# Order of wide and narrow matrix products in the chunks of a projection

## The chip, the cores and the metric

The kernel runs on one core of a Trainium2 chip. The metric is the device time of one execution in microseconds. The kernel before takes 881.99 us, the median of three runs (881.4 to 882.06). All engines start together, each works through its own queue in order, and they wait for each other by semaphores: TensorE (PE; its loading of weights is shown as PEld), VectorE (DVE), ScalarE (ACT), GpSimd (POOL) and SyncE (SP), which issues the transfers.

## The reference

The reference is an encoder of two layers on 256 tokens of width 1024, in float32. Each layer has a token mixer and a gated MLP:

```
def _token_mixer(xn, ...):
    u, q, k, v, g_pool, g_attn = jnp.split(xn @ w_in, SPLITS, axis=-1)
    ...
    pool_out = jnp.einsum('bsgc,gcd->bsgd', pooled, w_pool).reshape(B, S, POOL_WIDTH) * pool_scale
    ...
    merged = jax.nn.sigmoid(g_pool) * (pool_out @ w_a) + jax.nn.sigmoid(g_attn) * (attn_out @ w_b)
    return merged @ w_o

def _conv_ffn(xn, w_up, conv_w, conv_b, w_down):
    a, gval = jnp.split(xn @ w_up, 2, axis=-1)
    ...
    return (jax.nn.gelu(a) * gval) @ w_down

for layer in range(DEPTH):
    h = h + _token_mixer(_rmsnorm(h, norm1[layer]), ...)
    h = h + _conv_ffn(_rmsnorm(h, norm2[layer]), ...)
return _rmsnorm(h, norm_f)
```

Nearly all the work is the products of the 256 tokens with the weights.

## The kernel before

Float32 products are made of reduced-precision ones. Every operand is split into a high part, rounded to the format that TensorE multiplies (`fp32r`), and a low part, what the rounding left. A product is then three: high weight by high operand, high weight by low operand, low weight by high operand.

**Weights.** The class `Weights` loads them from HBM in 1 MB tiles (`raw`, three buffers, SP's queue), and cuts each tile into two pieces. `open_next` splits a piece: ACT casts the raw piece to `wh` (L177), DVE subtracts to get `wl` (L178), each 128x1024. `wh` and `wl` have five buffers each, and a piece is split when the piece three before it is taken (`LOOK = 3`, in `get`). A buffer of `wh` is free again when the last product that reads it is done, one of `wl` likewise.

**Projections.** `proj` (L479) takes one piece, 128 output channels by 1024 inputs, and one PSUM buffer of four (`mm`). Its operand `x2` holds for each of eight groups of 128 input channels the high part of the 256 tokens and the low part next to each other, so one product of 512 columns makes the high and the low one at once. `two_sums` (L471) does the whole chunk: eight wide products, 128x512, with the high weights (L475), into both halves of the PSUM buffer, and then eight narrow ones, 128x256, with the low weights and the high part of the operand (L477), added to the second half:

```
for k in range(nk):
    nc.tensor.matmul(ps, wh(k), x2[:, k], start=(k == 0), stop=False)
for k in range(nk):
    nc.tensor.matmul(ps[:, 1], wl(k), x2[:, k, 0], start=False, stop=(k == nk - 1))
```

The first product of a sum writes the buffer (`start`), all others add. The two halves are added together when the sum is read: `add_up` (L497 on ACT, L498 on DVE), or the lines of the queries and keys (L957 to L969).

`two_sums` is called 224 times in all, 112 per layer: 96 times by `proj` with `nk = 8`, for the pooling input, queries and keys, the projection `w_a` (operand `po2`), the gates, and the two halves of the MLP's input; 8 times in `pool_out` with `nk = 2` (`pool_ps`); 8 times for `w_b` with `nk = 4` (`b_ps`).

**Other work on TensorE.** The values (`v_sum`) and the output projections (`residual_mm`, `res_ps`, L502 to L504) have the roles turned round: weights stream as 512 columns, and all their products are wide. The attention has small products: scores (`s_ps`, 256 and 128 columns), transposes of the softmax rows (`pt_ps`, L901, 128 columns) and the weighted values (`o_ps`). They are put between the chunks of the last queries and keys and of `w_a`.

**What sets the order.** The text of the kernel is the program order. A scheduler puts the instructions of each engine into that engine's queue, by its own estimate of when each could run, and adds the semaphores. So an edit on TensorE can also change the order in which casts, subtractions and evictions stand on ACT and DVE. Each queue is then worked off strictly in order.

Of the kernel before, what the change touches and what calls it, by code (L numbers as in the profile page):

```python
# [204 lines left out]
def encoder(ctx, tc, x, w_in, w_pool, pool_scale, w_a, w_b, w_o, norm1, norm2, w_up, conv_w,  # L205
            conv_b, w_down, rel_bias, norm_f, onehot, edges, out):
    nc = tc.nc
# [255 lines left out]
    def store(t, r, xn):  # L463
# [4 lines left out]
        nc.sync.dma_start(out=ov[:, t, 512:], in_=xn[:, 512:])  # L468
        yield

    def two_sums(ps, wh, wl, x2, nk):  # L471


        for k in range(nk):
            nc.tensor.matmul(ps, wh(k), x2[:, k], start=(k == 0), stop=False)  # L475
        for k in range(nk):
            nc.tensor.matmul(ps[:, 1], wl(k), x2[:, k, 0], start=False, stop=(k == nk - 1))  # L477

    def proj(x2):  # L479

        i, (wh, wl) = W.get()
        ps = mmp.tile([P, 2, S], F32, tag="mm", name="proj_ps")
        two_sums(ps, lambda k: wh[:, k, :], lambda k: wl[:, k, :], x2, KD)
        W.free(i)
        return ps[:, 0], ps[:, 1]

    def halves(a):

        return a.rearrange("p (t m) -> p t m", t=2)
# [74 lines left out]
    def v_tile():  # L564
        return acc.tile([P, 512], F32, tag="acc", name="v_ps")
# [11 lines left out]
    def two_parts(tag, name):  # L577


        return big.tile([P, KD, 2, 2, P], F32R, tag=tag, name=name)  # L580
# [123 lines left out]
    def first_values(rs, raw_x, fs, done, pe, keep_values):  # L704

        xuh, xul = raw_x
        x2 = two_parts("x", "x2")

        rows = mmp.tile([P, 2, P], F32, tag="mm", name="r_ps")
        with tc.issue_after(pe.ins):  # L710
            for t in range(2):
                nc.tensor.transpose(rows[:, t, :], rs[t][:, 0:1].to_broadcast([P, P]), ident)
        for k in range(0, KD, 2):
            f = fs[k // 4][:, k % 4 : k % 4 + 2]
            for j in range(2):
                nc.vector.scalar_tensor_tensor(
                    out=f[:, j], in0=f[:, j], scalar=gcol[:, k + j : k + j + 1], in1=rows,
                    op0=ALU.mult, op1=ALU.mult,
                )
            oh, ol = (x2[:, k : k + 2, part] for part in (0, 1))  # L720
            nc.scalar.copy(out=oh, in_=f)
            nc.vector.tensor_sub(out=ol, in0=f, in1=oh.bitcast(F32))
        ps = done
        for g in range(NG):
            held = [W.get() for _ in range(4)] if g + 1 < NG else []
            for t in range(2):
                keep_values(t, g, ps[t], rs)
            ps = [v_tile() for _ in range(2)]
            for t in range(2):
                for n, (_, (wh, wl)) in enumerate(held):  # L730
                    for j in range(2):
                        k = 2 * n + j
                        for m, (a, w) in enumerate(((xuh, wh), (xuh, wl), (xul, wh))):
                            nc.tensor.matmul(  # L734
                                ps[t], a[:, k, t, :], w[:, j, :], start=(k + m == 0),
                                stop=(k == KD - 1 and m == 2),
                            )
            for i, _ in held:
                W.free(i)
        return x2  # L740

    for l in range(DEPTH):
# [21 lines left out]
        if l == 0:  # L764
            with tc.manual_schedule():
                begun = begin_values_of_x()
            x2 = first_values(*begun, keep_values)
        else:
            for g in range(NG):
                held = begun[0] if g == 0 else [W.get() for _ in range(4)]  # L770
                for t in range(2):
                    if g + t == 0:
                        ps = begun[1]
                    else:
                        ps = v_tile()
# [17 lines left out]
        for gi in range(3, -1, -1):  # L793
            w = WINDOWS[gi]
# [7 lines left out]
            cur, n = u, S + 2 * PAD  # L802
            sh = 1
            while sh < w:
# [3 lines left out]
                    out=nxt[:, :, 0:n], in0=cur[:, :, 0:n], in1=cur[:, :, sh : sh + n]  # L808
# [7 lines left out]
            if hw > 1:  # L816
# [5 lines left out]
                out=pd, in0=cur[:, :, o : o + S], scalar=1.0 / w, in1=u[:, :, PAD : PAD + S],  # L822
# [8 lines left out]
        def pool_out(po2):  # L831
            for j in range(2):
                i, (wh, wl) = W.get()
                for gg in range(2):
                    for oc in range(2):
                        ps = mmp.tile([P, 2, S], F32, tag="mm", name="pool_ps")
                        cc = slice(oc * P, (oc + 1) * P)
                        two_sums(
                            ps, lambda k: wh[:, 2 * gg + k, cc], lambda k: wl[:, 2 * gg + k, cc],
                            pooled[2 * j + gg], 2,  # L840
                        )
                        c = 4 * j + 2 * gg + oc
                        sc = hps[:, l, c : c + 1]
                        po = sm.tile([P, 2, P], F32, tag="u", name="po")
                        nc.scalar.mul(out=po, in_=halves(ps[:, 1]), mul=sc)
                        nc.vector.scalar_tensor_tensor(
                            out=po, in0=halves(ps[:, 0]), scalar=sc, in1=po, op0=ALU.mult, op1=ALU.add
                        )
                        nc.scalar.copy(out=po2[:, c, 0], in_=po)
                        nc.vector.tensor_sub(out=po2[:, c, 1], in0=po, in1=po2[:, c, 0].bitcast(F32))  # L850
                    if gg:
                        W.free(i)
                    yield
# [76 lines left out]
        steps = []  # L930
# [10 lines left out]
        for m, c in enumerate(PAIRS):  # L941
# [7 lines left out]
            for n in range(4):  # L949
                if m == 1:  # L950
                    next(pool_parts)
                src, rest = (halves(a) for a in proj(x2))
                hd = 2 * c + n % 2
                scale = HD**-0.5 if n < 2 else 1.0
                if hd < HPG:
# [3 lines left out]
                        out=lo[:, hd], in0=src, scalar=scale, in1=hi[:, hd].bitcast(F32),  # L959
# [3 lines left out]
                        out=lo[:, hd], in0=rest, scalar=scale, in1=lo[:, hd].bitcast(F32),  # L963
                        op0=ALU.mult, op1=ALU.add,
                    )
                else:
# [3 lines left out]
                        out=o, in0=src, scalar=scale, in1=o, op0=ALU.mult, op1=ALU.add  # L970
# [20 lines left out]
        for c in range(KD):  # L991
            th = gate(c)
            nc.vector.scalar_tensor_tensor(
                out=pa[:, c, :], in0=th, scalar=1.0, in1=pa[:, c, :], op0=ALU.add, op1=ALU.mult
# [3 lines left out]
        for c4 in range(2):  # L998
            ths = [gate(4 * c4 + j) for j in range(4)]
            for j2 in range(2):  # L1000
                i, (wh, wl) = W.get()
                for j in range(2):
                    c = 4 * c4 + 2 * j2 + j
                    ps = mmp.tile([P, 2, S], F32, tag="mm", name="b_ps")
                    cc = slice(j * P, (j + 1) * P)
                    two_sums(ps, lambda k: wh[:, k, cc], lambda k: wl[:, k, cc], at2, 4)
                    m = sm.tile([P, S], F32, tag="u", name="m")
                    add_up(m, (ps[:, 0], ps[:, 1]))
                    nc.vector.scalar_tensor_tensor(
                        out=m, in0=ths[2 * j2 + j], scalar=1.0, in1=m, op0=ALU.add, op1=ALU.mult  # L1010
                    )
                    nc.vector.tensor_add(out=m, in0=m, in1=pa[:, c, :])
                    m = halves(m)
                    nc.scalar.copy(out=mh[:, c], in_=m)
                    nc.vector.tensor_sub(out=ml[:, c], in0=m, in1=mh[:, c].bitcast(F32))
                W.free(i)

        x2 = two_parts("x", "x2")
# [41 lines left out]
        held, ps = entry  # L1060
        first = keep_entry(ps)
        ps = v_tile()
# [70 lines left out]
        if l + 1 < DEPTH:  # L1133
            x2 = two_parts("x", "x2")
# [34 lines left out]
```

## Time and profile before

| | |
|---|---|
| time, median of three runs | 881.99 us |
| time of the profiled execution | 882.08 us |
| span in its profile | 880.3 us |
| TensorE busy | 872.4 us, 99% |
| weight loads busy | 757.5 us, 86% |
| DVE busy | 682.5 us, 78% |
| ACT busy | 525.6 us, 60% |
| GpSimd busy | 14.0 us, 2% |
| mean share of the transfer engines (q1) | 56.0% |
| granted TensorE clock | 0.999 |

A line of a group reads: line of the kernel, engine, operation, what is written and read with shapes, count; then busy time in us and the mean ns of one; then the idle time of the engine just before them and what ended most of it. A line of the timeline reads: start in us from the span's start, length in us, engine, line, operation, tiles, count; neighbouring instructions of the same line are merged to one. Products on TensorE overlap, so the length of one is more than the distance from its start to the start of the next.

### The profile page before, as it was taken

How to read it: one execution, taken by the hardware profiler on the slowest of the kernel's cores; microseconds unless marked ns; L12 is line 12 of the kernel's file. 1: busy time of each engine (PE TensorE's matmuls, PEld its weight loads, DVE VectorE, ACT ScalarE, POOL GpSimd, SP SyncE). 2: the span in 40 equal slices, each digit the busy share in tenths (PEclk: the TensorE clock that was granted, in tenths of full speed). 3: DMA queues.
4: the chain of work that ended last, by engine and by line, in shares of the span. 5: the costliest groups of instructions: out<-in, count | busy, mean ns of one | idle time of the engine just before them, and what ended most of it. 6: DMA issues, size and time to landing. Idle time of an engine off the chain costs nothing.

```text
span 880.3 us, 12800 instructions
## 1 busy us (share of the span) xinstructions
PE 872.4 (99%) x4817; PEld 757.5 (86%) x4817; DVE 682.5 (78%) x1167; ACT 525.6 (60%) x929; POOL 14.0 (2%) x40
## 2 busy tenths in 40 slices
PE   9999999999999999999999999999999999999996
PEld 7888889988888888888888888999888888888885
DVE  6988886767869987787755987776678698878774
ACT  6746654556648766666545574554566486666652
POOL 2000000000000000000000000000000000000000
PEclk9999999999999999999999999999999999999999
DMA  9669744455554665465636465443556447566541
GB/s 327 233 204 313 240 144 147 141 181 176 175 207 147 205 225 193 155 221 198 239 120 220 163 199 185 148 163 124 191 189 205 159 146 257 167 197 205 172 144 50
DMA packets 125791, 164.48 MB, mean 187 GB/s; under 512 B 2995, under 2 KB 106107, under 8 KB 125600
## 3 DMA queue, kind: packets, MB, share of 16 engines
q1 hardware_dynamic: 125712, 163.65, 56.0%
q8 instruction: 38, 0.62, 0.3%
q14 instruction: 25, 0.20, 0.1%
q10 hardware_dynamic: 16, 0.00, 0.0%
HBM read 162.57 MB, written 3.69 MB: 189 GB/s over the span
## 4 chain that ended last, share of the span: by engine, by line
PE 99%; ACT 0%; POOL 0%; DVE 0%; issue 0%; POOLq 0%; ACTq 0%
PE proj_ps L475 40%; PE proj_ps L477 21%; PE res_ps L502 6%; PE v_ps L572 6%; PE res_ps L503 6%; PE res_ps L504 6%; PE v_ps L734 2%; PE b_ps L475 2%; PE v_ps L647 1%; PE b_ps L477 1%; PE pool_ps L475 1%; PE o_ps L922 1%; PE s_ps L872 1%; PE pt_ps L901 1%; PE s_ps L867 1%; PE o_ps L918 1%
## 5 line engine op out<-in xcount | busy, mean ns | idle before, releaser
L178 DVE TENSOR_TENSOR wl<-raw,wh 128x1024 fp32r<-128x1024 f32 x274 | 334.2, 1223 | 132.8 <-ACT wh L177 128.2
L177 ACT CAST wh<-raw 128x1024 fp32r<-128x1024 f32 x274 | 286.0, 1049 | 189.4 <-PE proj_ps L475 128.4
L475 PE MATMUL proj_ps<-x,wh 128*128 128x512 f32 x1408 | 354.1, 393 | 0.0
L475 PEld LDWEIGHTS proj_ps<-x,wh 128*128 128x128 f32 x1408 | 254.1, 189 | 47.3 <-issue 0.5
L477 PEld LDWEIGHTS proj_ps<-x,wl 128*128 128x128 f32 x1408 | 192.0, 190 | 13.8
L477 PE MATMUL proj_ps<-x,wl 128*128 128x256 f32 x1408 | 196.3, 282 | 0.0
L502 PE MATMUL res_ps<-wh,actq 128*128 128x512 f32 (+1 forms) x184 | 70.2, 381 | 0.0
L503 PE MATMUL res_ps<-wl,actq 128*128 128x512 f32 (+1 forms) x184 | 70.1, 381 | 0.0
L504 PE MATMUL res_ps<-wh,actk 128*128 128x512 f32 (+1 forms) x184 | 69.9, 380 | 0.0
L504 PEld LDWEIGHTS res_ps<-wh,actk 128*128 128x128 f32 x184 | 34.6, 188 | 6.7
L502 PEld LDWEIGHTS res_ps<-wh,actq 128*128 128x128 f32 x184 | 34.7, 188 | 6.2
L503 PEld LDWEIGHTS res_ps<-wl,actq 128*128 128x128 f32 x184 | 34.7, 188 | 6.0
L475 PE MATMUL proj_ps<-po,wh 128*128 128x512 f32 x128 | 33.1, 400 | 0.0
L1099 ACT ACTIVATE y<-y 128x256 f32<-128x256 f32 x44 | 18.3, 416 | 24.7 <-DVE y L1096 24.5
L1082 ACT ACTIVATE y<-a,prm 128x256 f32<-128x256 f32 x36 | 21.6, 600 | 15.9 <-DVE a L498 15.9
L416 ACT ACTIVATE junk<-h 128x512 f32<-128x512 f32 (+1 forms) x20 | 10.9, 546 | 27.0 <-DVE h L414 27.0
L502 PE MATMUL res_ps<-wh,m 128*128 128x512 f32 (+1 forms) x72 | 26.5, 368 | 0.0
L475 PEld LDWEIGHTS proj_ps<-po,wh 128*128 128x128 f32 x128 | 22.9, 189 | 4.1
L503 PE MATMUL res_ps<-wl,m 128*128 128x512 f32 (+1 forms) x72 | 26.3, 366 | 0.0
L504 PE MATMUL res_ps<-wh,m 128*128 128x512 f32 (+1 forms) x72 | 26.3, 365 | 0.0
L572 PE MATMUL v_ps<-wh,x 128*128 128x512 f32 x80 | 25.7, 392 | 0.0
L1083 DVE SCALAR_TENSOR_TENSOR y<-a,prm,y 128x255 f32<-128x255 f32 x36 | 17.3, 480 | 8.1 <-ACT y L1082 8.1
(208 smaller groups left out, 1101.6 us busy)
## 6 DMA issues: line engine op xcount, KB each, us to landing
raw<-in_w_in_dram SPq DMA_DIRECT2D x58, 1024.0 KB, 5.7
raw<-in_w_up_dram SPq DMA_DIRECT2D x44, 1024.0 KB, 4.9
raw<-in_w_down_dram SPq DMA_DIRECT2D x22, 1024.0 KB, 4.7
raw<-in_w_a_dram SPq DMA_DIRECT2D x8, 1024.0 KB, 5.3
raw<-in_w_o_dram SPq DMA_DIRECT2D x8, 1024.0 KB, 4.9
raw<-in_w_b_dram SPq DMA_DIRECT2D x4, 1024.0 KB
sk<-fd SPq DMA_DIRECT2D x1, 2560.0 KB
raw<-in_w_pool_dram SPq DMA_DIRECT2D x2, 1024.0 KB
```

What stands on the lines that cost most here:

```text
L177: lambda: nc.scalar.copy(out=h, in_=src),
L178: lambda: nc.vector.tensor_sub(out=l, in0=src, in1=h.bitcast(F32)),
L475: nc.tensor.matmul(ps, wh(k), x2[:, k], start=(k == 0), stop=False)
L477: nc.tensor.matmul(ps[:, 1], wl(k), x2[:, k, 0], start=False, stop=(k == nk - 1))
L502: nc.tensor.matmul(ps, ah, wh, start=first, stop=False)
L503: nc.tensor.matmul(ps, ah, wl, start=False, stop=False)
L504: nc.tensor.matmul(ps, al, wh, start=False, stop=last)
L572: nc.tensor.matmul(ps, x2[:, 2 * n + j, part, t, :], w[:, j, :], start=(n + m == 0), stop=(n == 3 and m == 5),)
L734: nc.tensor.matmul(ps[t], a[:, k, t, :], w[:, j, :], start=(k + m == 0), stop=(k == KD - 1 and m == 2),)
L1082: nc.scalar.activation(y, a, AF.Identity, bias=b, scale=w1)
L1083: nc.vector.scalar_tensor_tensor(out=y[:, 1:], in0=a[:, : S - 1], scalar=w0, in1=y[:, 1:], op0=ALU.mult, op1=ALU.add)
L1099: nc.scalar.activation(y2, y2, AF.Tanh, scale=c)
```

## The change

Only `two_sums` is changed. A flag that lives outside it turns over with every call. In the first, third, fifth call the order is as before. In every second call the order is: the first wide product, which opens the sum, then all narrow ones, then the remaining wide ones. The products, their operands and the buffers are the same; the last product of the sum, which ends it, is a wide one in these calls. All products of both kinds now stand on one line, L484, and the lines below move by seven.

```diff
+    turns = {"rest": False}
+
     def two_sums(ps, wh, wl, x2, nk):
...
-        for k in range(nk):
-            nc.tensor.matmul(ps, wh(k), x2[:, k], start=(k == 0), stop=False)
-        for k in range(nk):
-            nc.tensor.matmul(ps[:, 1], wl(k), x2[:, k, 0], start=False, stop=(k == nk - 1))
+        steps = [(k, True) for k in range(nk)]
+        rests = [(k, False) for k in range(nk)]
+        steps = steps[:1] + rests + steps[1:] if turns["rest"] else steps + rests
+        turns["rest"] = not turns["rest"]
+        for n, (k, wide) in enumerate(steps):
+            out, w, x = (ps, wh, x2[:, k]) if wide else (ps[:, 1], wl, x2[:, k, 0])
+            nc.tensor.matmul(out, w(k), x, start=(n == 0), stop=(n == 2 * nk - 1))
```

## The prediction

> **What bounds the kernel now.** I read the page first: busy times, the chain that ended last, the costliest groups.
>
> ```profile
> PE 872.4 (99%) x4817; PEld 757.5 (86%) x4817; DVE 682.5 (78%) x1167; ACT 525.6 (60%) x929; POOL 14.0 (2%) x40
> ...
> PE 99%; ACT 0%; POOL 0%; DVE 0%; issue 0%; POOLq 0%; ACTq 0%
> ...
> L178 DVE TENSOR_TENSOR wl<-raw,wh 128x1024 fp32r<-128x1024 f32 x274 | 334.2, 1223 | 132.8 <-ACT wh L177 128.2
> L177 ACT CAST wh<-raw 128x1024 fp32r<-128x1024 f32 x274 | 286.0, 1049 | 189.4 <-PE proj_ps L475 128.4
> L475 PE MATMUL proj_ps<-x,wh 128*128 128x512 f32 x1408 | 354.1, 393 | 0.0
> ```
>
> The chain is TensorE from end to end, and the products sit behind no idle time: the last column of the L475 group is 0.0. So the end is the sum of the distances from one product's start to the next one's. The 393 ns is the length of one, not its distance: products overlap. Distances have to be read from starts, in the timeline of TensorE. This is the MLP stage, where a chunk is eight wide products (L475) and eight narrow ones (L477):
>
> ```profile
> 325.88 1.98 PE L475 MATMUL proj_ps<-x,wh 128*128 128x512 f32 x8
> 327.69 1.12 PE L477 MATMUL proj_ps<-x,wl 128*128 128x256 f32 x8
> 328.64 2.00 PE L475 MATMUL proj_ps<-x,wh 128*128 128x512 f32 x8
> 330.48 1.11 PE L477 MATMUL proj_ps<-x,wl 128*128 128x256 f32 x8
> ...
> 337.02 0.40 PE L502 MATMUL res_ps<-wh,actq 128*128 128x512 f32 x1
> ...
> 338.18 0.39 PE L504 MATMUL res_ps<-wh,actk 128*128 128x512 f32 x1
> ...
> 342.26 0.39 PE L504 MATMUL res_ps<-wh,actk 128*128 128x512 f32 x1
> ```
>
> The eight wide ones at 325.88 follow another wide one and take 327.69 - 325.88 = 1.81 us, 226.7 ns each in the unrounded starts. The next eight follow narrow ones and take 330.48 - 328.64 = 1.84. So a wide stretch costs 27 ns more behind narrow products. The residual rows show where: behind narrow ones the first five steps (337.02 to 338.18) take 1.16 us, 1.133 at the steady pace; the next 18 (to 342.26) take 4.08, which is 226.7 each. Unrounded, the surpluses of the first five are 6.5, 9, 1.5, 5.5 and 4.5 ns. A narrow stretch is the reverse: its first product is 113 ns from the second, the second 119, the rest 120; eight take 0.95 us.
>
> What happens behind few products of a kind, in the stage of the pooled projection and in that of the bias table:
>
> ```profile
> 79.26 0.62 PE L475 MATMUL pool_ps<-pl,wh 128*128 128x512 f32 x2
> 79.72 0.40 PE L477 MATMUL pool_ps<-pl,wl 128*128 128x256 f32 x2
> 79.96 2.00 PE L475 MATMUL proj_ps<-x,wh 128*128 128x512 f32 x8
> 81.80 1.12 PE L477 MATMUL proj_ps<-x,wl 128*128 128x256 f32 x8
> ```
>
> ```profile
> 44.80 1.11 PE L477 MATMUL proj_ps<-x,wl 128*128 128x256 f32 x8
> 45.84 0.28 PE L374 MATMUL f_ps<-onehot_r,rh 33*4 33x256 f32 x1
> ...
> 48.11 1.11 PE L477 MATMUL proj_ps<-x,wl 128*128 128x256 f32 x8
> 49.15 0.28 PE L374 MATMUL f_ps<-onehot_r,rh 33*4 33x256 f32 x1
> ```
>
> Two narrow products are enough for the full surplus: the wide eight at 79.96 take 1.84 again. Two wide ones behind narrow ones take 79.72 - 79.26 = 0.46, 0.453 at the steady pace: a short stretch pays only its own first positions. And eight narrow ones take 1.04 us to the next group whether one wide product stands before them (44.80) or eight (48.11).
>
> **The change part by part.** In every second sum the wide stretch of eight becomes one wide product, eight narrow, seven wide. Products, operands and bytes stay the same in number.
>
> *The pace of TensorE.* Two chunks in a row go from 8 wide, 8 narrow, 8 wide, 8 narrow to 8 wide, 8 narrow, 1 wide, 8 narrow, 7 wide, and the 7 run on into the next chunk's 8. The number of meetings of sizes is the same, but of two full wide stretches behind narrow ones (2 x 27.4 ns) one shrinks to a single product (6.5 ns): 21 ns less per pair. I counted the stretches in the two kernels' instruction lists, over proj_ps, pool_ps and b_ps. Wide stretches behind narrow, before: 166 of five or more (27.4 ns), 16 of four (22.3, the b_ps rows), 16 of two (12.6, mean of the pool_ps rows), 1 of one: 4.55 + 0.36 + 0.20 + 0.01 = 5.11 us. After: 110 of five or more, 4 of three (17), 105 of one (6.5): 3.01 + 0.07 + 0.68 = 3.76. That is -1.35 us. Stretches behind the 128-wide products of the attention (36 ns net for eight, 6 for one, 10 for two): eight full ones become single and two more of two appear, -8 x 36 + 8 x 6 + 2 x 10 = -0.22 us. Narrow stretches behind a wide product go from 229 to 243, each with 8 ns of quick start: -0.11. Eight more groups of 128-wide products stand behind a wide one, which costs about 12 ns in the starts: +0.10. Sum: **-1.6 us**.
>
> Unknown is the lone wide product between two narrow stretches; no 8-8-1-8 order is in the trace. Bound below: it runs at the steady pace, 105 x 6.5 = 0.7 us more gain, -2.3. Bound above: the narrow eight behind it lose their quick start, 112 x 8 = +0.9, so -0.7. I take the middle value, since the nearest rows (0.46 for two wide ones; 1.04 behind one wide or eight) show neither deviation.
>
> The Trainium skill, "TensorE: Matmul & The Clock Gate", section "Back-to-back issue gap", gives the distance of isolated products as columns over 2.4 GHz plus 2.5 ns, so by each product's own size alone; by it a sum doesn't depend on the order, and the time would stay. The trace disagrees: 1.81 and 1.84 us for the same eight.
>
> *Narrow weights needed sooner.* In the 112 changed sums the product with wl starts 7 x 0.23 = 1.6 us (chunks of eight) earlier. The tightest such chunk:
>
> ```profile
> 289.97 1.22 DVE L178 TENSOR_TENSOR wl<-raw,wh 128x1024 fp32r<-128x1024 f32 x1
> 297.26 1.12 PE L477 MATMUL proj_ps<-x,wl 128*128 128x256 f32 x8
> ```
>
> Its subtraction ended at 291.19, 6.1 us ahead; 4.5 remain. Cost nothing, either way: pieces are split three ahead, one per 2.79 us. Had DVE no lead, each late piece would cost TensorE its lateness.
>
> *Buffers and sums.* A changed sum releases wh at its end instead of 0.95 us before, so the cast (L177, ACT) for five pieces later can start up to 0.95 us later, with what stands behind it on ACT (evictions of sums) and with the subtraction on DVE. wl is released sooner by up to 1.8 us. Readers that begin with the first half of the sum (L957) also wait 0.95 us longer, though the sum as a whole ends as before. These delays meet the PSUM buffers: the tightest is pool_ps at 91.12, which DVE freed (L969, started 89.56) 1.14 us before. Covered, so nothing; without that cover up to 0.95 us at a place.
>
> *Queues.* SP (180 entries) and POOL (40) keep their order, so no transfer moves. On ACT casts move by -2 to +4 places, on DVE subtractions by -13 to +10, among work with the leads above. On TensorE two groups of four transposes, one per layer (L901, 119.27 and its repeat), get two products of the next sum between them; the second group waits for a softmax row that was ready 0.4 us before, so this adds slack. Nothing there.
>
> The profiled execution took 882.08 us (span 880.3 and 1.8 around it), 0.1 above the median, 881.99. The forecast is 881.99 - 1.6 = **880.4 us**.
>
> **The rivals.** *The lone wide product is free*: 2.3 us gain, 879.7. For it: the surplus of a first product is 6.5 of 27 ns; against: every first wide product behind a narrow one shows it.
>
> *The order is free*: the surplus belongs to the narrow work, is only booked on the wide products and goes with its amount; 882.0. Against: two narrow ones cause as much as eight (79.96). This is also what the skill's formula gives.
>
> *Unpaid surplus is carried*: the 21 ns that a lone wide product doesn't pay fall on the narrow ones behind it, +2.2 us, and the quick start is lost too, +0.9: 883.5. Against: 1.04 us in both rows at 44.80 and 48.11.
>
> *Slower, by the split chain*: the later cast. DVE is busy 78%, and L178 waits 128 us for the casts, those 128 us for L475. If the 0.95 us of each changed chunk adds up instead of being made up in the idle time, the 4.5 us of lead are gone after five changed chunks and each further one costs TensorE 0.95; four of them make 884.2. Against: the idle time, 189 us on ACT before this very cast.
>
> **How the numbers follow.** Forecast 0.64, with its own range 879.7 to 881.3; free lone product 0.16; order free 0.05; carried 0.03; split chain 0.12. 0.2% is 1.76 us, about what a measurement of this kernel can tell from none. That bound, 880.2, cuts the forecast's range: I give 0.28 of its 0.64 to faster and 0.36 to within. Faster 0.28 + 0.16 = 0.44; same 0.36 + 0.05 + 0.03 = 0.44; slower 0.12. Range 879.2 to 882.6: it leaves out the split chain, the carried case and the tail of the free one.
>
> **What would show it.** In the timeline a pair of chunks: 1 wide to the first narrow 0.23, eight narrow 0.95, seven wide 1.61, the next eight wide 1.81 (1.84 before). The chain stays TensorE 99%, idle 0.0 before the products, span near 878.7. Wrong if the eight wide behind seven wide still take 1.84 or the narrow ones behind a lone wide take over 0.96 (pace), or if wl by L178 or a PSUM reader shows up as releaser of TensorE (a wait).

## The result, and the profile after

The changed kernel takes 880.43 us (median of 22 runs, 880.09 to 882.06); the kernel before, run beside it, 881.66 us (22 runs). The ratio is 0.9984, with a 95% interval of 0.9978 to 0.9991: 1.2 to 1.4 us faster, where 1.6 had been forecast. The profiled execution has a span of 878.7 us. In the runs of the experiments two executions took several times as long as the rest (3090.93 us of `e7_opened_ahead`, 4571.08 of the kernel before), and the ratios leave them out.

The page of the changed kernel, the lines that answer to those shown of before (busy times, chain, groups):

```profile
PE 870.6 (99%) x4817; PEld 756.5 (86%) x4817; DVE 684.3 (78%) x1167; ACT 524.1 (60%) x929; POOL 14.1 (2%) x40
...
PE 99%; ACT 0%; issue 0%; POOL 0%; DVE 0%; POOLq 0%; ACTq 0%
...
L178 DVE TENSOR_TENSOR wl<-raw,wh 128x1024 fp32r<-128x1024 f32 x274 | 334.0, 1223 | 87.1 <-ACT wh L177 85.0
L484 PE MATMUL proj_ps<-x,wh 128*128 128x512 f32 x1408 | 360.0, 393 | 0.0
L177 ACT CAST wh<-raw 128x1024 fp32r<-128x1024 f32 x274 | 286.4, 1050 | 80.4 <-PE res_ps L511 39.1
```

TensorE is still the whole chain, and this view shows no idle time before the products. The casts wait less before them than before (80 us instead of 189), and other lines of ACT wait more (L1089, which was L1082, 40 us instead of 16); none of it is on the path.

The timeline of TensorE in the MLP stage of the changed kernel, at the place shown before:

```profile
325.00 1.98 PE L484 MATMUL proj_ps<-x,wh 128*128 128x512 f32 x8
326.82 1.11 PE L484 MATMUL proj_ps<-x,wl 128*128 128x256 f32 x8
327.77 0.40 PE L484 MATMUL proj_ps<-x,wh 128*128 128x512 f32 x1
328.00 1.12 PE L484 MATMUL proj_ps<-x,wl 128*128 128x256 f32 x8
328.96 3.59 PE L484 MATMUL proj_ps<-x,wh 128*128 128x512 f32 x15
332.39 1.12 PE L484 MATMUL proj_ps<-x,wl 128*128 128x256 f32 x8
333.34 0.40 PE L484 MATMUL proj_ps<-x,wh 128*128 128x512 f32 x1
```

From start to start: the lone wide product takes 0.23 us, the narrow eight behind it 0.96 (0.95 behind a long stretch), the fifteen wide ones 332.39 - 328.96 = 3.43, which is 15 x 226.7 ns and 0.03 us more, once for two sums. Before, each eight paid that 0.03 by itself.

Not all of the 1.6 us between the two profiles (880.3 and 878.7 us) is the change. The first projection starts at 42.37 us in the profile of before and at 41.70 in this one, though TensorE's products ahead of it are the same. The two timelines of TensorE part in the warm-up; the kernel before first, then the changed one:

```profile
5.11 1.06 PE L333 MATMUL warm_ps<-ones 128*128 128x128 f32 x4
5.97 0.80 PE L647 MATMUL v_ps<-m,xuh 128*128 128x512 f32 x1
```

```profile
5.12 0.71 PE L333 MATMUL warm_ps<-ones 128*128 128x128 f32 x4
5.98 0.50 PE L654 MATMUL v_ps<-m,xuh 128*128 128x512 f32 x1 [0.15 <-ACT m L185]
```

The same products are slow for longer in the first: the pace doubles at 7.4 us there, at 5.3 here, where TensorE even waits for ACT (0.15 us). So below I compare the time from the first projection's first product to the last product of all, which leaves the start out: 831.0 us before, 830.0 with the change. On that measure the change is worth 1.0 us in these two profiles.

### The profile page after: what moved, and what is told of

Same layout as the page of the kernel before. It is cut to its first block, busy times and chain, and to the rows that moved or that the text cites. A ratio compares the mean times of both kernels' runs of the same rounds, so it can differ in the third digit from the quotient of the medians.

```text
span 878.7 us, 12698 instructions
## 1 busy us (share of the span) xinstructions
PE 870.6 (99%) x4817; PEld 756.5 (86%) x4817; DVE 684.3 (78%) x1167; ACT 524.1 (60%) x929; POOL 14.1 (2%) x40
## 4 chain that ended last, share of the span: by engine, by line
PE 99%; ACT 0%; issue 0%; POOL 0%; DVE 0%; POOLq 0%; ACTq 0%
PE proj_ps L484 61%; PE v_ps L579 6%; PE res_ps L510 6%; PE res_ps L511 6%; PE res_ps L509 6%; PE b_ps L484 3%; PE v_ps L741 2%; PE v_ps L654 1%; PE pool_ps L484 1%; PE s_ps L879 1%; PE o_ps L929 1%; PE pt_ps L908 1%; PE s_ps L874 1%; PE o_ps L925 1%; PE xt_ps L450 1%; PE gain_ps L333 0%
## 5 line engine op out<-in xcount | busy, mean ns | idle before, releaser
L484 PE MATMUL proj_ps<-x,wh 128*128 128x512 f32 x1408 | 360.0, 393 | 0.0
L484 PEld LDWEIGHTS proj_ps<-x,wh 128*128 128x128 f32 x1408 | 257.5, 188 | 47.3 <-issue 0.7
L484 PEld LDWEIGHTS proj_ps<-x,wl 128*128 128x128 f32 x1408 | 192.6, 190 | 10.6
L484 PE MATMUL proj_ps<-x,wl 128*128 128x256 f32 x1408 | 196.7, 283 | 0.0
L1089 ACT ACTIVATE y<-a,prm 128x256 f32<-128x256 f32 x36 | 21.6, 601 | 40.3 <-DVE a L505 40.3
L484 PE MATMUL proj_ps<-po,wh 128*128 128x512 f32 x128 | 34.0, 400 | 0.0
L484 PEld LDWEIGHTS proj_ps<-po,wh 128*128 128x128 f32 x128 | 23.1, 189 | 3.9
L995 ACT ACTIVATE gates<-gates 128x256 f32<-128x256 f32 x32 | 13.1, 415 | 18.9 <-DVE gates L505 18.9
```

The lines of the kernel that those rows point to most:

```text
L484: nc.tensor.matmul(out, w(k), x, start=(n == 0), stop=(n == 2 * nk - 1))
L995: nc.scalar.activation(th, th, AF.Tanh, scale=0.5)
L1089: nc.scalar.activation(y, a, AF.Identity, bias=b, scale=w1)
```

## The experiments

My theory is the prediction's: the end is TensorE's pace, a wide product behind narrow ones pays by its place in its stretch, and no wait comes in. The rivals: each meeting of sizes has one price; the gain comes from shifted buffers and queues; the surplus has to do with something narrow products lack time for.

"Surplus" is the distance from one start to the next over 226.7 ns for a wide product and 113.3 for a narrow one; means over the sums of a kind, from 60 us on.

**Every sum turned round** (`e1_every_sum`).

```diff
-        steps = steps[:1] + rests + steps[1:] if turns["rest"] else steps + rests
+        steps = steps[:1] + rests + steps[1:]
```

> Every sum, not every second one, has the order one wide, eight narrow, seven wide. The narrow weights are wanted early and the high weights released late in all 224 sums, but the sizes follow each other as in the kernel before: the seven run on into the next sum's one, so stretches of eight wide and eight narrow take turns again. Theory (the gain is the pace of TensorE by stretch length, nothing else): a wide eight takes 1.84 us in the timeline, the time is that of before, 881.7 us, ratio 0.9995 to 1.0007. Rival (the gain comes from the shifted releases of buffers and the changed queues on ScalarE and VectorE): the same gain as with the change or twice it, 880.4 to 879.2 us. Rival (lone wide products are what helps): also a gain.

Measured: 883.84 us, ratio 1.0021 (1.0012 to 1.0030). No gain, so turning round as such brings nothing; but slower by 0.2%, which my theory did not expect. The pace is that of before: wide eights take 1841 ns between starts, as before, narrow ones 953 against 952. The loss is waits. The two longest of TensorE's waits behind 60 us, as its weight loads show them, and the place of the second in its timeline:

```profile
PEld proj_ps L484 <- DVE po L853: 0.9, 1, 0.9
PEld xt_ps L450 <- DVE xn L441: 0.7, 1, 0.7
```

```profile
440.96 0.28 PE L511 MATMUL res_ps<-wh,actk 128*128 128x256 f32 x1
441.53 0.41 PE L450 MATMUL xt_ps<-ident,xn 128*128 128x128 f32 x2 [0.29 <-DVE xn L441]
442.43 0.44 PE L450 MATMUL xt_ps<-ident,xn 128*128 128x128 f32 x2 [0.49 <-DVE xn L441]
```

At 441 us DVE is late with the norm (1.1 us lost), at 88 us with freeing a PSUM buffer (0.8), and in both attentions with a softmax row (0.3 each): 2.5 us in all, against 2.7 more from first projection to last product (833.7).

The two large places have different histories. At 441 us it is the chain of buffers. Counted from the start of the first projection, the transfer of a weight tile (the one that the cast waits for, by the order of the transfers) is issued at 389.2 us, in the kernel before at 386.0; the tile is cast at 394.5 instead of 392.0, and the eviction that the norm needs stands on DVE behind the subtraction that waits for this cast. At 88 us a weight tile lands late, and with it come late the cast, the subtraction and the instruction that frees the buffer (`po`, L853):

```profile
85.33 1.05 ACT L177 CAST wh<-raw 128x1024 fp32r<-128x1024 f32 x1 [1.57 <-DMA raw<-in_w_in_dram]
86.41 1.23 DVE L178 TENSOR_TENSOR wl<-raw,wh 128x1024 fp32r<-128x1024 f32 x1 [2.11 <-ACT wh L177]
87.89 0.48 DVE L853 SCALAR_TENSOR_TENSOR po<-pool_ps,hps,po 128x256 f32<-128x256 f32 x1
```

The same cast waits 1.52 us for its tile in `e3_opening_in_halves`, where only every second sum is turned round, and TensorE loses 0.5 us there; in the changed kernel it waits 0.77 and TensorE loses 0.2 us at 87.4 us, and in a second profile of it (`e9_change_again`) 0.29 and nothing is lost. The tile's transfer is issued 36.2 us after the start of the first projection in this run, 36.2 and 34.8 in the two profiles of the changed kernel, 34.3 and 35.7 in those of the kernel before, so it moves by as much between runs of one kernel as between kernels. So the rival "split chain and buffers" is a real price where every sum is turned round, at 441 us; that the 0.8 us at 88 us belong to the order is not shown.

**One by one** (`e2_take_turns`).

```diff
-        steps = steps[:1] + rests + steps[1:] if turns["rest"] else steps + rests
+        steps = [(k, wide) for k in range(nk) for wide in (True, False)]
```

> Wide and narrow products take turns one by one in every sum: the most meetings of sizes that there can be, and nearly only lone wide ones. Theory (a wide product behind a narrow one pays by its place in its stretch, 6.3 ns for the first of up to 28 for five; a narrow product behind one wide one 3.7 ns over 113.3): 8 x (6.3 + 3.7) = 80 ns of surplus per sum of 16, against 73 of before: +7 x 192 sums = +1.3 us, 883 us, ratio 1.0005 to 1.0025. Rival (each meeting of a narrow and a wide product costs the same 20 ns or more, whatever the stretch): seven more meetings per sum, 7 x 192 x 20 ns = +27 us, 908 us.

Measured: 885.85 us, ratio 1.0044 (1.0031 to 1.0056). The price per meeting is far from constant: seven more meetings per sum cost 4.5 us in the profile, not 27. But 1.3 was worked out. Waits are 0.9 of it, the rest is pace: the wide ones stand 234.7 ns apart and the narrow ones 116.8, so 8 x (8.0 + 3.5) = 92 ns per sum, not 80. A surplus read from a first product in a long order was too small for an order that has only such products.

**The opening product in halves** (`e3_opening_in_halves`).

```diff
-        steps = steps[:1] + rests + steps[1:] if turns["rest"] else steps + rests
...
+        if turns["rest"]:
+            for a in (0, 1):
+                nc.tensor.matmul(ps[:, a], wh(0), x2[:, 0, a], start=(a == 0), stop=False)
+            steps = rests + steps[1:]
+        else:
+            steps = steps + rests
...
```

> In every second sum the wide product that opens it is made as two products of 256 columns, one for each half, with the same weights; then the narrow ones, then the other wide ones. No lone wide product is left: stretches of 18 narrow and 15 wide, and half as many meetings as before. 112 products of 128x512 become 224 of 128x256. Theory (narrow ones cost 7 ns over their streaming from the third of a stretch on, full wide stretches 28.5): per two sums 28.5 + 6 + 16 x 6.7 = 142 to 146 ns of surplus against 146 before and 132 with the change: 881.3 to 881.7 us, so the halved meetings gain nothing, ratio 0.9990 to 1.0005. Rival (what counts is the number of meetings, and the lone wide product is a cost): more gain than the change, -2 us, 879.6 us or less, ratio 0.9977.

Measured: 882.2 us, ratio 1.0001 (0.9993 to 1.0010), as the theory has it. Half as many meetings gain next to nothing when they are bought with products of 256 columns: two of those stand 240 ns apart where one wide takes 226.7. From first projection to last product it takes 831.15 us, as before; 0.5 of that is the wait at 88 us, so the pace alone gains 0.3 to 0.5 us, where 0 to 0.4 had been worked out.

**Narrow products of 320 columns** (`e4_narrow_320`), in the kernel before.

```diff
-            nc.tensor.matmul(ps[:, 1], wl(k), x2[:, k, 0], start=False, stop=(k == nk - 1))
+            if nk == KD:
+                out = ps.rearrange("p a m -> p (a m)")[:, 192:512]
+                x = x2[:, k].rearrange("p a t m -> p (a t m)")[:, 0:320]
+            else:
+                out, x = ps[:, 1], x2[:, k, 0]
+            nc.tensor.matmul(out, wl(k), x, start=False, stop=(k == nk - 1))
```

> The kernel before, with the eight narrow products of a projection's sum made 320 columns wide instead of 256: they stream 64 columns of the low part more and add them into the last 64 columns of the first half, so the sums are not those of the reference. Theory (a narrow product streams in 113.3 ns but follows the next only at 120, since something per product, such as the load of its weights, takes 120; this lag is what the first five wide ones pay for): 320 columns stream in 141.7 ns, longer than 120, so there is no lag: the narrow ones stand 141.7 ns apart from the first on, and the wide eight behind them take 1.81 us instead of 1.84. Time: 192 x (1.134 - 0.952) = +34.9 us and about 160 x 27.4 ns = -4.4 us less surplus: 912 us. Rival (every change of size costs the wide ones their 27 ns): 1.84 us remain, 916.6 us.

Measured: 922.73 us in one run. Its timeline in the MLP stage:

```profile
326.21 2.00 PE L475 MATMUL proj_ps<-x,wh 128*128 128x512 f32 x8
328.05 1.33 PE L482 MATMUL proj_ps<-x,wl 128*128 128x320 f32 x8
329.22 2.00 PE L475 MATMUL proj_ps<-x,wh 128*128 128x512 f32 x8
```

The theory of this experiment falls. The wide eight still take 328.05 - 326.21 = 1.84 us (1838 ns, against 1841 behind 256 columns), and the 320-column ones stand 146.5 ns apart, not 141.7. So it is not a fixed 120 ns per product that holds the narrow ones back. The distances fit one line instead. From 256 to 512 columns they grow from 120 to 226.7 ns, which is 0.417 ns per column or 2.4 GHz; at that rate 256, 320 and 512 columns take 106.7, 133.3 and 213.3 ns, and 13.3 ns are left at 256 and 512, 13.2 at 320. The Trainium skill, "TensorE: Matmul & The Clock Gate", section "Back-to-back issue gap", has the same form for isolated products, with 2.5 ns in place of the 13.3; the measurement decides. What the surplus of the wide ones is, stays open: it goes with the change of size, and wider narrow ones did not remove it.

**Two and four wide ones in front** (`e5_two_open`, `e6_four_open`).

```diff
-        steps = steps[:1] + rests + steps[1:] if turns["rest"] else steps + rests
+        steps = steps[:2] + rests + steps[2:] if turns["rest"] else steps + rests
```

`e6_four_open` has `nk // 2` in place of 2.

> In every second sum two wide products stand before the narrow ones instead of one, and six behind them. Theory (pace by place in the stretch): per two sums 13 ns for the two, about 47 for the narrow eight behind them, 28.5 for the long wide stretch, 45.6 for the other narrow eight: 134 ns of surplus against 146 before and 132 measured with one: -12 x 96 = -1.2 us of pace, and 0.2 us of waits as with the change: a gain of 0.9 to 1.2 us, 880.6 us. Rival (what helps is how early the narrow ones come): a gain between those of one and none, about the same; this run tells little between them, the next one does.

> Half of the wide products (four of eight) stand before the narrow ones in every second sum, four behind. Theory: four wide ones pay 23 of the full 27 ns, so per two sums 23 + 47 + 28.5 + 45.6 = 144 ns against 146: -0.2 us of pace, no gain that can be measured, ratio 0.9993 to 1.0005. Rival (joining the rest of the wide stretch to the next sum's is what helps, whatever the length of the opening stretch): the gain of the change, 0.16%, ratio 0.9984.

Measured: with two 878.94 us, ratio 0.9965 (0.9953 to 0.9978); with four 880.72 us, 0.9989 (0.9980 to 0.9998). Two in front gain twice what one does, and no wait stands in the profile. Their timelines, first with two, then with four:

```profile
326.93 0.63 PE L484 MATMUL proj_ps<-x,wh 128*128 128x512 f32 x2
327.39 1.10 PE L484 MATMUL proj_ps<-x,wl 128*128 128x256 f32 x8
328.33 3.36 PE L484 MATMUL proj_ps<-x,wh 128*128 128x512 f32 x14
331.53 1.11 PE L484 MATMUL proj_ps<-x,wl 128*128 128x256 f32 x8
332.49 0.63 PE L484 MATMUL proj_ps<-x,wh 128*128 128x512 f32 x2
```

```profile
327.66 1.09 PE L484 MATMUL proj_ps<-x,wh 128*128 128x512 f32 x4
328.59 1.11 PE L484 MATMUL proj_ps<-x,wl 128*128 128x256 f32 x8
329.54 2.91 PE L484 MATMUL proj_ps<-x,wh 128*128 128x512 f32 x12
```

The wide stretches pay what was worked out (0.46 us for two, 3.20 for fourteen). It is the narrow eight behind the two that are quicker: 328.33 - 327.39 = 0.94 us. Over all such sums the narrow eight take 957 ns behind one wide product, 939 behind two, 946 behind four, 952 behind eight or more. So the pace of a narrow stretch also depends on the stretch before it, and not in one direction. The theory had no such term, and with four it missed: 0.2 us of pace had been worked out, 1.0 to 1.2 came. The rival's ratio (0.9984) lies within the interval of the four, but the profiles show the narrow stretches as the larger part of the gain (0.6 us).

**The next sum opened ahead** (`e7_opened_ahead`). The core of the edit, in `proj`:

```diff
+        if opened:
+            c = opened.pop()
+            narrow(c, False)
+            wide(c, range(1, KD), True)
+        else:
+            c = take()
+            wide(c, range(KD))
+            if opens:
+                opened.append(take())
+                wide(opened[0], (0,))
+            narrow(c, True)
```

> Where two sums of the same operand follow each other, the wide product that opens the second is put behind the eight wide ones of the first, ahead of the first one's narrow ones: 9 wide, 8 and 8 narrow, 7 wide that run on into the next pair. No lone wide product, the same products, half as many meetings of sizes. Single sums, the pooled projection and the projection w_b stay as in the kernel before. Theory: per pair 28.5 + 99 = 127 ns of surplus against 146 before and 132 with the change, for about 88 pairs: -1.7 us of pace against before, 0.5 better than the change; with no new wait 879.9 us, ratio 0.9980. Rival (the earlier opening and the later release of buffers make waits, as with every sum turned round): the gain of pace is eaten, 880.5 to 882 us.

Measured: 880.70 us in the ten runs that the ratio uses, ratio 0.9985 (0.9976 to 0.9994). In the profile the pace does what the theory says: 829.45 us from first projection to last product, 1.5 to 1.7 less than before, without a wait after 60 us. The measured time gains less than that, 0.9 us in the medians and 1.3 by the ratio; the interval holds both, so whether some of the gain is lost outside the pace stays open.

**The kernel before, the change and the version with two once more** (`e8_before_look`, `e9_change_again`, `e10_two_again`; no new edit).

> The kernel before once more, for its profile. Its first profile starts the first projection 0.67 us later than the others do (42.37 against 41.70 us), all of it in the first 8 us. Theory (that is the start-up of TensorE, which differs from run to run, and no part of the change): the first projection starts anywhere from 41.6 to 42.5 us, and from there to the last product it takes 831.0 us again, within 0.1, without a wait after 60 us. Rival (the change itself moves the start): 42.37 us again.

> The changed kernel once more, beside the version with two opening wide products on the same chip. Theory (pace): from the first projection to the last product 830.0 us in the profile against 831.0 to 831.1 before, ratio 0.9980 to 0.9992.

> Two wide products open every second sum, once more. Theory: the gain of its first run was pace, since no wait stood in its profile: narrow eight behind a lone pair of wide ones take 939 ns, not 952 or 957. The profile repeats that, 828.5 us from the first projection to the last product, ratio 0.9960 to 0.9978, faster than the change on the same chip. Rival (a lucky profile): 830 us and the ratio of the change.

Measured: the kernel before starts its first projection at 41.93 us this time and takes 831.13 us from there; the change 42.07 and 829.82, ratio 0.9986 (0.9977 to 0.9996); two in front 41.88 and 828.46, ratio 0.9971 (0.9961 to 0.9982), 879.13 us. Over all fourteen profiles the start lies between 41.58 and 42.37 us, whatever the kernel. So the start is not the change's, and the change's pace is worth 1.0 to 1.3 us; the version with two in front is faster than the change in both of its runs.

**Three in front, and pairs that take turns** (`e11_three_open`, `e12_pairs_take_turns`).

```diff
-        steps = steps[:1] + rests + steps[1:] if turns["rest"] else steps + rests
+        steps = steps[:3] + rests + steps[3:] if turns["rest"] else steps + rests
```

```diff
-        steps = steps[:1] + rests + steps[1:] if turns["rest"] else steps + rests
+        steps = [p for k in range(0, nk, 2) for p in steps[k : k + 2] + rests[k : k + 2]]
```

> Three wide products open every second sum. If the pace of the narrow ones goes smoothly with the length of the wide stretch before them (957, 939 and 946 ns behind 1, 2 and 4), they take about 942 ns behind three; the three wide ones pay 17 to 25 ns. Per two sums 20 + 35 + 28.5 + 45.6 = 129 ns of surplus against 146 before: -1.6 us, ratio 0.9975 to 0.9987. If only an even number brings the quick pace, they take 952 to 957 ns: -0.5 us, ratio 0.9990 or more.

> In every sum two wide and two narrow products take turns. From the rows of the pooled projection, which has this order already (467 ns for two wide, 229 for two narrow): 4 x 696 = 2784 ns per sum against 2793 before, -9 x 192 = -1.8 us, 880 us, ratio 0.9975 to 0.9985, if the rows of a few products carry over to long repetition. Rival (they don't, as with one by one, where 3.65 us were lost in pace and 1.3 had been worked out): no gain or a loss of up to 2 us. Waits may come on top, since the narrow weights are wanted early in all sums: up to 1 us.

Measured: three in front 880.54 us, ratio 0.9988 (0.9979 to 0.9996); the narrow eight behind three take 949 ns, between the two cases, so the pace does not go smoothly with the length (957, 939, 949, 946). Pairs that take turns: 879.96 us, ratio 0.9978 (0.9969 to 0.9987); 466.3 ns for two wide ones and 230.6 for two narrow, so 697 where 696 had been read from the pooled projection's rows. Rows of the very order carry over to long repetition within 1 ns, and no wait came in. But four such pairs in each of 192 sums make of that 1 ns 0.7 us, and the profile gains 1.3 to 1.5 us (829.67), not the 1.8 worked out; the medians gain 2.0.

## Why the prediction was right, and where it was off

The way and the cause of the gain were right. That 880.43 us stands so near the 880.4 forecast is luck in part: the kernel before took 881.66 us beside it, 0.3 less than the 881.99 that the forecast started from, and the gain was that much smaller than forecast.

**The bound** held: TensorE is the chain, its distances make the time.

**The wide stretches** held. The table sets the terms of the sum against the profiles, from 60 us on, the change as in `e9_change_again`, which has no wait in that stretch:

| term | forecast, us | measured, us |
|---|---|---|
| wide stretches behind narrow | -1.35 | -1.24 |
| around the 128-wide products | -0.22 + 0.10 | -0.40 |
| narrow stretches | -0.11 | +0.53 |
| sum | -1.58 | -1.11 |

**The step that was off** is the narrow eight behind a lone wide product: "I take the middle value, since the nearest rows (0.46 for two wide ones; 1.04 behind one wide or eight) show neither deviation". They do lose their quick start, as the bound above had it: 957 ns against 952, and the stretches of two and four in the pooled projection and in w_b likewise (238 ns against 231, 482 against 474). Of the 0.9 us put down for that loss, 0.64 came. The rows that misled were those at 44.80 and 48.11: their stretches stand between the products of the bias table, which have 33 rows, and there one wide product and eight give the same to the nanosecond; between sums they don't.

**Around the 128-wide products** it gained more than forecast, which hides part of that loss. The eight groups of transposes that now stand behind a wide product cost about 5 ns each, not 12, and the wide eight behind groups of transposes pay 101 ns over their pace on the mean, not 124 as before; why, stays open.

**The lone wide product** paid 6.3 ns, as taken (6.5).

**The narrow weights needed sooner**: no product waited for wl in the steady part; held. **Buffers**: nearly held. The place named as the tightest, `pool_ps` at 91.12 us, cost the change nothing. But 3 us ahead of it a PSUM buffer came 0.2 us late in one of its two profiles, released by DVE (L853): by the prediction's own list a sign of being wrong, though a small one. It came behind a cast that had waited 0.77 us for its weight tile.

**The rivals.** *Order is free* and *unpaid surplus is carried* fall with the result; *the lone wide product is free* falls with its 6.3 ns. *Slower, by the split chain* did not come with every second sum. With every one there are 2.5 us of waits, of which the 0.8 behind a late weight tile are not shown to come from the order. Its mechanism as I put it, 0.95 us that add up over a stage, is not what was seen; single places with little slack gave way.

## What to carry to other kernels

Where TensorE never waits, the time is the sum of start-to-start distances, and these depend on the order of sizes: read them from starts, by the place in a stretch and by the stretch before it, and expect changes of tenths of a per cent. Terms read from rows of the very order carried over to a long run within 1 ns in 697, and even that 1 ns is a large part of so small a gain; terms put together from neighbours were off by 5 to 15 ns per narrow stretch, so small variants of such an order (two in front instead of one) have to be run, not only reasoned about. And a turn that is nearly free in every second sum can cost waits in every sum, where it takes slack from places that have little, as at 441 us.

## What was not expected of the hardware

A product of fp32r with its own weights follows the one before by 0.417 ns per column plus 13.3 ns (120, 146.5 and 226.7 ns for 256, 320 and 512 columns), once its stretch has settled (for 256 columns, behind eight or more products of 512). After a change to 512 columns the first five products take 27 ns more in all behind 256 columns, 25 behind 320. Narrow eights take 957, 939, 949, 946 and 952 ns behind 1, 2, 3, 4 and 8 wide products. The length is not all: behind six wide ones the two sums that have this order take 958 ns with two in front (`e5_two_open`, `e10_two_again`) and 949 with four. Why, stays open.

The warm-up of TensorE at the start of an execution ended anywhere from 4.5 to 7.4 us, by the clock records of the fourteen traces. Where it ended by 5.9 us, the first projection starts at 41.58 to 41.73 us; where it ended later, at 41.88 to 42.37. These 0.8 us are more than half of what the change is worth, while the profiles' mean clock reads 0.997 to 0.999 throughout. The Trainium skill, "TensorE: Matmul & The Clock Gate", section "What's actually happening", tells of an activity window that runs freely and so ends the slow start at another time in each run, within 0.5 us either way. The fourteen traces agree that the end moves, but it moves by more, 2.9 us between the first and the last.
